# A decoder block on one core: the first weight groups of each half in another order

## The chip, the core and the metric

The kernel runs on one core of one Trainium2 chip. Its engines are TensorE (PE in the rows, with PEld for its weight loads), VectorE (DVE), ScalarE (ACT), GpSimd (POOL) and SyncE (SP), which here only issues transfers. The metric is device time in microseconds, the median of the runs; a profiled execution of the same program gives the trace. In the rows, "A<-B" is an instruction or a transfer that writes tile A and reads B. The kernel records nearly all its instructions through one helper, so the line is L56 almost everywhere, and one goes by the tiles' names.

## What is computed

A decoder trunk of one layer on 2048 tokens of width 1024, in float32:

```python
u = x * (1.0 + scale) + shift                      # from SiLU(c) @ w_ada + b_ada
q, k, v, a_gate, p_in, p_gate, m_a, m_p = split(u @ w_in)
a = sliding_window_sink_attention(q, k, v, ...) * silu(a_gate)
a = a @ w_attn_proj
p = einsum('bsgc,gcd->bsgd', multiscale_causal_pool(p_in), w_pool_mix)
p = ((p * pool_scale) * silu(p_gate)) @ w_pool_proj
y = sigmoid(m_a) * a + sigmoid(m_p) * p
y = (y @ w_out) * (1.0 + gate)
x = layer_norm(alpha * x + y)
```

16 query heads of 64 share two key and value heads; the window is 128 tokens.

## The kernel before

*Products.* Every large matrix product goes in blocks of two by two, with seven products of half-size blocks in place of eight (class `Quad`: two weight tiles of 128 output columns, one chunk of 1024 tokens). The seven are named after the token-side operand: B11, T1, T2, B21, T3, B22, T4. Each float32 operand is split into a high and a low part, and each product is 12 matmuls of 128 x 512 (four blocks, three matmuls each). The weight-side sums are made on GpSimd (`sum1`, `mid`, `late`) and stored to a DRAM tensor `sums_d` in chunk 0 (`keep_sum`); in chunk 1 a quad that has such sums (`again`) loads them instead.

*Order.* Nothing is scheduled by the machine: `phases` lists groups of one or two quads, `plan` turns them into a fixed list of products, and `run` emits them. A group of two runs F (B11, T1 of the first, then of the second), S (T2, B21), Th (T3, B22) and L (T4): 14 products. The two groups of a start phase are thus products 0 to 13 and 14 to 27. After a product's results are complete, `consume(ph, mi, t, src)` is called for one tile of 128 x 512 (output tile `mi`, token half `t`): for the first quad of a pair after products 5, 8, 9 and 12 of the group, for the second after 7, 10, 11 and 13. `defer(2, f)` puts `f`, mostly a store, into program order two products later, and `at(p, f)` hangs other work at product p. Every engine, and SP's queue of transfers, works in program order.

*The start phases.* For each of the two chunks of 1024 tokens (s = 0, 1) a phase with two pairs comes first: `g0` and `g1`. In `g0` the function `head` first makes the modulation and the token-side operands while the data arrives, and does the F and S products of the first pair by hand along the way; so the second quad of the first pair never calls `keep_sum` there, and has no kept sums in chunk 1 either. Between products 10 and 25 of `g0` the function `fold_parts` puts 16 small products (12 matmuls of 128 x 256, into the banks `pv` and `pt` in turn) which fold the pooling weights: ScalarE copies each result to a tile `st`, SP stores it to `wmix_d`. `gate_modulation` fetches 16 half rows of weights (`room_small`) and reduces them on VectorE; its last store is `gate_d`, 4 KB in pieces of 4 bytes.

*What the consumers use.* They take tiles from a ring `c` of the phase (`ph.c`): four tiles in `g0`, six in `g1`. In `g0` the head takes three of them for rows of x. A tile can be written again when the store that reads it has landed.

- `kv_quad`: keys into halves of `spare`, values through a transpose; no tile of `c`.
- `q_quad`: two tiles (`q_hi` on ScalarE, `q_lo` on VectorE), two stores of 256 KB to `q_d`.
- `gate_quad`: one tile `sig` (tanh on ScalarE, and one VectorE instruction for the two gates that are SiLU), one store of 256 KB to `gates_d`, in the rows `ag_d` (attention) and `pg_d` (pooling).

*After the start.* Phase `o0` or `o1` runs 13 quads one at a time and lays attention over them, in steps called every few matmuls. On entry it loads keys (`kk`), the first query tile (`qs`, from `q_d`), the bias (`bt`) and the values (`vv`); later steps load one further query tile for every two steps.

Of the kernel before, what the change touches and what calls it, by code (L numbers as in the profile page):

```python
# [36 lines left out]
TQ, TK, TV, TAG, TPG, TMA, TMP = 0, 8, 9, 10, 18, 26, 34  # L37
# [22 lines left out]
def kernel(  # L60
# [77 lines left out]
    sums_d = dp.tile([36, P, 2, CH], F32, name="sums_d")  # L138
    y_d = dp.tile([S // P, P, KT, P], F32, name="y_d")

    def cols(t, n):
        return t[:, n * CH : (n + 1) * CH]
# [4 lines left out]
    def as32(ap):  # L147
        return ap.bitcast(F32)

    def low(engine, dst, src, hi):  # L150
        engine.tensor_tensor(dst, src, as32(hi), ALU.subtract)
# [9 lines left out]
    def bank(tag="mm"):  # L161
        if tag in ("c1", "pv"):
            return phase_ps["now"].tile([P, CH], F32, tag=tag, bufs=phase_ps["pv"] if tag == "pv" else 1, name=tag)
        return ps.tile([P, CH], F32, tag=tag, bufs=4 if tag == "mm" else 1, name=tag)
# [148 lines left out]
    def defer(ticks, f, local=False):  # L313
        due.append((now[0] + ticks, len(due), f, local))
# [231 lines left out]
    def kv_quad(s):  # L546
        def keep_k(ph, t, src):
            hi, lo = ph.pair()
            act.copy(hi, src)
            low(dve, lo, src, hi)  # L550
            defer(2, lambda: [sp.dma_start(cols(k_d[s, :, n, :], t), as32(x)) for n, x in enumerate((hi, lo))])

        def turn_v(ph, t, vt):
            vtp = bank(("pv", "pt")[t]).rearrange("p (b a d) -> p b a d", b=NB, a=2)
            for b in range(NB):
                pe.transpose(vtp[:, b].rearrange("p a d -> p (a d)"), vt[:, b * P : (b + 1) * P], ident)
            v = ph.two_halves()
            hi, lo = (v.rearrange("p (a b n d) -> p n b a d", a=2, b=NB, n=2)[:, n] for n in range(2))
            act.copy(hi, vtp)
            low(dve, lo, vtp, hi)  # L560
            v = as32(v).rearrange("p (a b d) -> p a b d", a=2, b=NB)
            defer(2, lambda: [sp.dma_start(v_d[s, :, a, NB * t : NB * (t + 1)], v[:, a]) for a in range(2)])

        def consume(ph, mi, t, src):
            if mi == 0:
                keep_k(ph, t, src)
            else:
                vt = ph.own("vt") if s == 0 else cols(ph.spare(), 0)
                act.activation(vt, src, AF.Copy, scale=0.5)
                defer(2, lambda: turn_v(ph, t, vt))  # L570

        return Quad((win[TK], win[TV]), consume)

    def q_quad(s, m):
        def consume(ph, mi, t, src):
            hi, lo = ph.c("q_hi", F32R), ph.c("q_lo", F32R)
            act.activation(hi, src, AF.Copy, scale=-0.125)
            dve.scalar_tensor_tensor(lo, src, -0.125, as32(hi), ALU.mult, ALU.subtract)
            defer(2, lambda: [sp.dma_start(q_d[s, m + mi, t, n], as32(x)) for n, x in enumerate((hi, lo))])

        return Quad((win[TQ + m], win[TQ + m + 1]), consume, sums_d[1 + m // 2], s == 1)

    def gate_quad(s, name, base, m, full):
        def consume(ph, mi, t, src):
            g = ph.c("sig")
            act.activation(g, src, AF.Tanh, scale=0.5)
            if full:
                dve.scalar_tensor_tensor(g, g, 1.0, src, ALU.add, ALU.mult)
            defer(2, lambda: sp.dma_start(gates_d[name][s, m + mi, t], g))

        kept = () if base + m == TAG else (sums_d[5 + (base + m - TAG) // 2], s == 1)
        return Quad((win[base + m], win[base + m + 1]), consume, *kept)

    def mix_quad(s, m):
        def consume(ph, mi, t, src):
            x = ph.c("px")
            act.activation(x, src, AF.Copy, scale=psc[:, m + mi : m + mi + 1])
            defer(2, lambda: sp.dma_start(px_d[m + mi, :, (2 * s + t) * CH : (2 * s + t + 1) * CH], x))

        return Quad(tuple(wmix_d[m + i].rearrange("p k d -> p (k d)") for i in range(2)), consume, sums_d[21 + m // 2], s == 1)  # L600
# [560 lines left out]
    def chunk_quads(s):  # L1161
        def gates(name, base, full):
            return {m: gate_quad(s, name, base, m, full) for m in range(0, KT, 2)}

        q = {m: q_quad(s, m) for m in range(0, KT, 2)}
        x = {m: mix_quad(s, m) for m in range(0, KT, 2)}
        ag, pg = gates("ag", TAG, True), gates("pg", TPG, True)
        ma, mp = gates("ma", TMA, False), gates("mp", TMP, False)
        start = [[kv_quad(s), ag[0]], [q[0], pg[0]]]
        alone = [q[2], ag[2], x[0], x[2], q[4], ag[4], x[4], q[6], ag[6], x[6], pg[2], ma[0], ma[2]]  # L1170
        end = [[pg[4], pg[6]], [ma[4], ma[6]], [mp[0], mp[2]], [mp[4], mp[6]]]
        return start, [[z] for z in alone], end
# [272 lines left out]
    for s in range(2):  # L1445
        start, alone, end = chunk_quads(s)
        if s == 0:
            phase(Pools("g0", spare=2, x=3), start, first_start)
        else:
            phase(Pools("g1", spare=5, wx=2, c=6, ux=2), start, second_start)  # L1450
        phase(Pools(f"o{s}", pv=2, wx=1, p=1, c=5 if s else 4, ux=1), alone, middle(s))
        phase(Pools(f"e{s}", pg=2, wx=2 if s else 3, c=6, ux=1), end, finish_chunk(s, ain_d[0] if s else u1_d))
# [63 lines left out]
```

## Time and profile before

| | |
|---|---|
| median of 3 runs | 1749.45 us (1749.2 to 1755.33) |
| profiled execution, its own time | 1751.48 us |
| its span, first to last instruction | 1749.7 us |
| mean granted TensorE clock | 0.985 |
| TensorE busy | 1672.3 us, 96% of the span |
| VectorE, ScalarE, GpSimd busy | 73%, 54%, 34% |
| transfers | 389.49 MB, mean 223 GB/s |

Busy time of TensorE counts matmuls as they lie in the pipeline, so 96% is not 96% of its peak; but idle time there is time in which the program's order found an operand or a bank not ready. In the profile's rows "idle before" an instruction is followed by what ended it last.

### The profile page before, as it was taken

To read this page: it belongs to the slowest core of one execution; us is meant where nothing else is said; L and a number is where in the kernel's file an instruction comes from. 1 tells how busy PE (TensorE), PEld (TensorE's weight loads), DVE (VectorE), ACT (ScalarE), POOL (GpSimd) and SP (SyncE) were. 2 spreads that over 40 slices of the span, in tenths; PEclk is the share of its full clock that TensorE was granted. 3 is DMA by queue.
4 is the path that set the end of the run, shared out by engine and by line. 5 is a ranking of instruction groups with operands and counts; after the bars stand their busy time and mean duration, and the time that the engine had idled before them with its cause. 6 is when DMAs were issued, how large, how long until landed. Compare 5 with 4: busy or idle time off the path is not lost.

```text
span 1749.7 us, 24770 instructions
## 1 busy us (share of the span) xinstructions
PE 1672.3 (96%) x8061; PEld 1398.1 (80%) x8061; DVE 1278.1 (73%) x2327; ACT 939.7 (54%) x1796; POOL 590.5 (34%) x562
## 2 busy tenths in 40 slices
PE   6889899999999999999999999999999999999996
PEld 5677688888888888888888888888888888888774
DVE  5855677778866778658787887487877785877677
ACT  3644577767763436347767676343545343445441
POOL 3022345454553323323334333322332211123442
PEclk9899999999999999999999999999999999999998
DMA  9388757776647888774556453589957786684342
GB/s 349 106 263 272 205 178 259 215 234 220 203 153 225 264 275 316 264 262 136 165 171 208 152 180 122 195 280 312 348 209 281 249 314 222 221 307 172 144 145 108
DMA packets 237713, 389.49 MB, mean 223 GB/s; under 512 B 21888, under 2 KB 91280, under 8 KB 237456
## 3 DMA queue, kind: packets, MB, share of 16 engines
q1 hardware_dynamic: 236368, 386.29, 66.2%
q10 hardware_dynamic: 1184, 1.60, 0.3%
q8 instruction: 63, 1.03, 0.2%
q14 instruction: 66, 0.54, 0.1%
q0 software_dynamic: 32, 0.02, 0.0%
HBM read 243.63 MB, written 147.35 MB: 223 GB/s over the span
## 4 chain that ended last, share of the span: by engine, by line
PE 63%; DVE 11%; DMA 7%; ACT 6%; issue 5%; POOL 1%; SPq 1%; POOLq 0%; DVEq 0%; ACTq 0%
PE mm L56 38%; PE lg L56 11%; PE c L56 9%; DVE w_set L56 3%; PE pv L56 3%; PE pt L56 2%; DVE L L56 2%; DVE wide L56 2%; ACT L L56 2%; ACT w_set L56 1%; SPq L56 1%; DMA qs<-q_d 1%; DMA wide<-in_xr_dram 1%; DVE p L56 1%; ACT sig L56 1%
## 5 line engine op out<-in xcount | busy, mean ns | idle before, releaser
L56 PE MATMUL mm<-set_B,w_set 128*128 128x512 f32 x2664 | 657.6, 394 | 1.1 <-DVE w_set L56 0.8
L56 PEld LDWEIGHTS mm<-set_B,w_set 128*128 128x128 f32 x2664 | 500.6, 190 | 105.6 <-DVE w_set L56 1.7
L56 POOL TENSOR_TENSOR W<-W 128x512 f32<-128x512 f32 x185 | 267.2, 1454 | 593.0 <-DVE w_set L56 411.6
L56 PE MATMUL mm<-set_T,w_set 128*128 128x512 f32 x1824 | 451.8, 394 | 0.7 <-DVE set_T L56 0.7
L56 PEld LDWEIGHTS mm<-set_T,w_set 128*128 128x128 f32 x1824 | 340.1, 190 | 71.1 <-DVE set_T L56 2.3
L56 DVE TENSOR_TENSOR w_set<-W,w_set 128x1024 fp32r<-128x1024 f32 x198 | 255.9, 1292 | 115.7 <-ACT w_set L56 112.5
L56 ACT CAST w_set<-W 128x1024 fp32r<-128x1024 f32 x222 | 232.1, 1047 | 82.2 <-PE mm L56 52.0
L56 ACT ACTIVATE L<-L 128x257 f32<-128x257 f32 (+3 forms) x384 | 191.2, 500 | 118.7 <-DVE L L56 118.0
L56 PE MATMUL lg<-set_T,w_set 128*128 128x512 f32 x864 | 213.3, 395 | 6.3 <-ACT w_set L56 3.6
L56 PE MATMUL c<-set_T,w_set 128*128 128x512 f32 x864 | 212.9, 395 | 5.1 <-ACT w_set L56 3.0
L56 PEld LDWEIGHTS lg<-set_T,w_set 128*128 128x128 f32 x864 | 163.2, 190 | 43.8 <-ACT w_set L56 4.8
L56 PEld LDWEIGHTS c<-set_T,w_set 128*128 128x128 f32 x864 | 163.3, 190 | 42.1 <-ACT w_set L56 4.6
L56 POOL TENSOR_TENSOR W<-W,A 128x512 f32<-128x512 f32 x41 | 58.0, 1415 | 278.1 <-DMA A<-in_win_dram 128.9
L56 DVE CUSTOM_DVE_ANT_0 L<-lg,bt,nsink 128x256 f32<-128x256 f32 (+1 forms) x256 | 111.0, 469 | 20.7 <-PE lg L56 14.5
L56 PEld LDWEIGHTS lg<-kk,qs 128*128 128x128 f32 x512 | 76.6, 189 | 43.0 <-DVE L L56 26.6
L56 PE MATMUL lg<-kk,qs 128*128 128x256 f32 (+1 forms) x512 | 83.5, 285 | 24.7 <-DVE L L56 18.1
L56 DVE TENSOR_TENSOR ptl<-pt,pth 128x512 fp32r<-128x512 f32 (+1 forms) x128 | 85.7, 670 | 28.8 <-ACT pth L56 27.8
L56 DVE TENSOR_SCALAR L<-L 128x256 f32<-128x256 f32 (+1 forms) x128 | 98.4, 769 | 4.5
L56 ACT ACTIVATE sig<-mm 128x512 f32<-128x512 f32 x76 | 45.5, 599 | 91.4 <-PE mm L56 86.8
L56 ACT CAST pth<-pt 128x512 fp32r<-128x512 f32 (+1 forms) x128 | 72.3, 565 | 20.1 <-PE pv L56 19.1
L56 POOL TENSOR_TENSOR w_set<-W,w_set 128x1024 fp32r<-128x1024 f32 x24 | 58.2, 2424 | 56.6 <-ACT w_set L56 35.3
L56 PE MATMUL pt<-ident,L 128*128 128x128 f32 x496 | 76.9, 277 | 0.0
(203 smaller groups left out, 1938.8 us busy)
## 6 DMA issues: line engine op xcount, KB each, us to landing
W<-in_win_dram SPq DMA_DIRECT2D x40, 512.0 KB, 5.9
qs<-q_d SPq DMA_DIRECT2D x128, 128.0 KB, 4.4
sums_d<-W SPq DMA_DIRECT2D x62, 256.0 KB, 4.0
W<-sums_d SPq DMA_DIRECT2D x31, 512.0 KB, 3.6
ain_d<-st SPq DMA_DIRECT2D x56, 256.0 KB, 3.8
A<-in_win_dram SPq DMA_DIRECT2D x42, 256.0 KB, 5.5
ag_d<-sig SPq DMA_DIRECT2D x32, 256.0 KB, 4.6
q_d<-q_hi SPq DMA_DIRECT2D x32, 256.0 KB, 3.7
```

Of the source, the lines that this page charges most:

```text
L56: return lambda *args, **kw: self.tc.keep_in_program_order(op(*args, **kw))
```

## The change

Each half's first four quads come in another order: the keys and values are paired with the first two query tiles, and the first tiles of both gates form the second pair. Before, keys and values were paired with the attention gate, and the queries with the pooling gate. So that the right sums are kept, the quad that now stands in the head (the queries) has none, and the attention gate's first quad keeps them in chunk 0 and reads them in chunk 1.

```diff
--- before.py
+++ after.py
@@ -578,7 +578,8 @@
             dve.scalar_tensor_tensor(lo, src, -0.125, as32(hi), ALU.mult, ALU.subtract)
             defer(2, lambda: [sp.dma_start(q_d[s, m + mi, t, n], as32(x)) for n, x in enumerate((hi, lo))])
 
-        return Quad((win[TQ + m], win[TQ + m + 1]), consume, sums_d[1 + m // 2], s == 1)
+        kept = (sums_d[1 + m // 2], s == 1) if m else ()
+        return Quad((win[TQ + m], win[TQ + m + 1]), consume, *kept)
 
     def gate_quad(s, name, base, m, full):
         def consume(ph, mi, t, src):
@@ -588,7 +589,7 @@
                 dve.scalar_tensor_tensor(g, g, 1.0, src, ALU.add, ALU.mult)
             defer(2, lambda: sp.dma_start(gates_d[name][s, m + mi, t], g))
 
-        kept = () if base + m == TAG else (sums_d[5 + (base + m - TAG) // 2], s == 1)
+        kept = sums_d[5 + (base + m - TAG) // 2], s == 1
         return Quad((win[base + m], win[base + m + 1]), consume, *kept)
 
     def mix_quad(s, m):
@@ -1166,7 +1167,7 @@
         x = {m: mix_quad(s, m) for m in range(0, KT, 2)}
         ag, pg = gates("ag", TAG, True), gates("pg", TPG, True)
         ma, mp = gates("ma", TMA, False), gates("mp", TMP, False)
-        start = [[kv_quad(s), ag[0]], [q[0], pg[0]]]
+        start = [[kv_quad(s), q[0]], [ag[0], pg[0]]]
         alone = [q[2], ag[2], x[0], x[2], q[4], ag[4], x[4], q[6], ag[6], x[6], pg[2], ma[0], ma[2]]
         end = [[pg[4], pg[6]], [ma[4], ma[6]], [mp[0], mp[2]], [mp[4], mp[6]]]
         return start, [[z] for z in alone], end
```

## The prediction

> **What bounds the kernel now.** I read the page first (busy shares), then what TensorE waits for, by stretch of the span, then the order of time in the two stretches where it waits, and last the windows, for clock and transfers.
>
> The page, its first line and TensorE's entry in part 1:
>
> ```profile
> span 1749.7 us, 24770 instructions
> PE 1672.3 (96%) x8061; PEld 1398.1 (80%) x8061; DVE 1278.1 (73%) x2327; ACT 939.7 (54%) x1796; POOL 590.5 (34%) x562
> ```
>
> TensorE runs 96% of the span, and the change adds and removes no matmul. So only TensorE's idle time, and slow running after it, can move the end. The waits of TensorE, four rows from three answers: the first 200 us, the rest, and the stretch from 686 to 768 us, where chunk 1 opens (engine, what it waited for, total, times, longest):
>
> ```profile
> PE lg L56 <- DMA qs<-q_d: 6.6, 1, 6.6
> PE pv L56 <- ACT st L56: 4.5, 1, 4.5
> PE pt L56 <- ACT st L56: 3.5, 1, 3.5
> ...
> PE lg L56 <- DVE L L56: 16.7, 17, 2.9
> ...
> PE lg L56 <- DVE set_T L56: 0.4, 1, 0.4
> ```
>
> The reader is to see that three single waits stand at the places the change touches: 6.6 at the first score tiles (queries not there), 4.5 in the first group of chunk 0, 3.5 in its second group. After 200 us the largest total is 16.7 in 17 small pieces inside attention, which the order of the start does not touch, and chunk 1's opening has 0.4 us in all, on a set split that stays.
>
> The second group of chunk 0, six rows of the timeline (start, length, engine, operation; in brackets the idle time before it and what ended it):
>
> ```profile
> 145.76 0.33 SPq L56 DMA_DIRECT2D room_small<-in_wada_dram  x1
> 146.14 0.42 SPq L56 DMA_DIRECT2D pg_d<-sig  x1
> 150.30 0.69 DVE L56 SCALAR_TENSOR_TENSOR q_lo<-mm,q_hi 128x512 fp32r<-128x512 f32 x1 [4.57 <-DMA pg_d<-sig]
> 152.66 0.43 SPq L56 DMA_DIRECT2D q_d<-q_hi  x1
> 156.43 0.63 ACT L56 ACTIVATE sig<-p 128x512 f32<-128x512 f32 x1 [8.22 <-DMA q_d<-q_hi]
> 157.58 2.62 PE L56 MATMUL pt<-spare,room_w 128*128 128x256 f32 x12 [3.55 <-ACT st L56]
> ```
>
> This is the ring of four "c" tiles. A query result takes two tiles of it (high and low part), a gate result one, and a tile comes back only when its store has landed. VectorE's q_lo waits 4.57 us for the store of a gate; with VectorE stuck, the fetch behind it on SP's queue is late, and so the next query store (152.66); ScalarE then waits 8.22 us for that store, and with it the copy "st" queued behind, which frees the PSUM bank of the next fold; TensorE idles 3.55 us. What follows it runs slowly. From the chain that ended last, a regular product and fold, then the two products after the stall:
>
> ```profile
> 122.02 2.75 PE lg L56 x12
> 124.77 1.43 PE pv L56 x12
> ...
> 160.20 3.36 PE lg L56 x12
> 163.56 2.73 PE c L56 x12
> ```
>
> **The change part by part.** Products of the two groups are numbered 0 to 27 as in the description above; results of the second member of a pair come at 7, 10, 11, 13 of a group, of the first at 5, 8, 9, 12.
>
> *Group 2 of chunk 0 (removes).* Before: 4 query results x 2 + 4 gate results = 12 tiles through a ring of 4. After: 8 gate results = 8 tiles. So 24 takes the tile of 19, 25 that of 21, 26 that of 22, 27 that of 23: four or five products, at the pace of 2.75 + 1.43 = 4.18 us a product at least 16.7 us, lie between. The tightest I can check in the rows is 25: the store at 146.14 is that of 21's result, it had landed when q_lo ran at 150.30, and product 25 ended at 157.58 - 3.55 = 154.03, so 3.7 us are to spare. I take the whole stall as gone: 3.55 idle, 2.62 - 1.43 = 1.19 on the fold, 3.36 - 2.75 = 0.61 on the product after it; the next one is back at 2.73. Sum **-5.35 us**. Bounds: 0 (another releaser takes over) and -5.35. What is late next: ScalarE's w_set for the following product; it was queued behind the same 8.22 us wait, so it moves with it.
>
> [...] These windows are length, then busy time and count of PE, PEld, DVE, ACT, POOL, granted clock, transfer share, GB/s:
>
> ```profile
> 96.00:100.00 4.00, 1.91 (x15) 1.63 (x13) 0.88 (x3) 0.60 (x1) 0.00 (x0) 1.00 1.02 375
> 156.00:160.00 4.00, 2.42 (x13) 2.42 (x13) 2.91 (x6) 3.54 (x6) 0.25 (x1) 0.75 0.44 137
> 168.00:192.00 24.00, 17.70 (x82) 14.38 (x80) 8.08 (x20) 7.87 (x17) 7.31 (x6) 0.93 1.04 212
> ```
>
> The clock falls to 0.75 in the slice of the stall, and by the chain's rows that costs 1.8 us. [...]
>
> *Group 1 of chunk 0 (adds).* Work on the engines: a query result is one ScalarE and one VectorE instruction, a gate result also. By shape, mean ns behind the bar:
>
> ```profile
> L56 ACT ACTIVATE sig<-mm 128x512 f32<-128x512 f32 x76 | 45.5, 599 | 91.4 <-PE mm L56 86.8 <-issue 4.0
> L56 ACT ACTIVATE q_hi<-mm 128x512 fp32r<-128x512 f32 x22 | 13.2, 599 | 26.5 <-PE mm L56 16.5 <-DMA q_d<-q_hi 9.7
> L56 DVE SCALAR_TENSOR_TENSOR sig<-sig,mm 128x512 f32<-128x512 f32 x40 | 27.5, 686 | 23.6 <-ACT sig L56 23.4
> L56 DVE SCALAR_TENSOR_TENSOR q_lo<-mm,q_hi 128x512 fp32r<-128x512 f32 x22 | 15.2, 692 | 37.8 <-ACT q_hi L56 33.2 <-DMA pg_d<-sig 4.6
> ```
>
> 599 against 599 and 692 against 686: nothing. Transfers (queue, KB each, us to landing, from the page):
>
> ```profile
> ag_d<-sig SPq DMA_DIRECT2D x32, 256.0 KB, 4.6
> q_d<-q_hi SPq DMA_DIRECT2D x32, 256.0 KB, 3.7
> ```
>
> Each of the four results now has two stores of 256 KB instead of one: four more on SP's queue in group 1, four fewer in group 2. Group 1 already has a stall:
>
> ```profile
> 93.95 0.52 SPq L56 DMA_DIRECT2D ag_d<-sig  x1
> 94.97 0.61 SPq L56 DMA_DIRECT2D sums_d<-W  x1
> 95.64 0.64 SPq L56 DMA_DIRECT2D wmix_d<-st  x1
> 96.52 0.60 ACT L56 ACTIVATE sig<-c 128x512 f32<-128x512 f32 x1 [2.25 <-PE c L56]
> 101.72 0.59 ACT L56 COPY st<-pv 128x512 f32<-128x512 f32 x1 [4.60 <-DMA wmix_d<-st]
> 102.36 1.11 PE L56 MATMUL pv<-ident,vt 128*128 128x128 f32 x4 [4.45 <-ACT st L56]
> ...
> 103.47 4.35 PE mm L56 x12
> ...
> DMA to landing us min/median/max: 5.7/5.7/5.7
> ```
>
> (the last row is the landing of the store at 93.95 alone). That store becomes two. The second issue, some 0.5 us, fits between 94.47 and 94.97, where SP waits, so wmix_d is issued no later; but it lands behind 256 KB more. 262,144 bytes at the 375 GB/s of the window from 96 to 100 are 0.70 us: **+0.70 us** on TensorE. Bounds: 0 (queue not full) and 1.4 (the extra store at product 7 still weighs too). The other three extra issues fall where SP waits for VectorE to free a buffer. The new wait in this group: the result of 13 takes tiles whose stores were issued at 93.95 and about 94.4; landing 5.7 later, plus 0.7 behind its own double, by 100.8. ScalarE has only the copy at 101.72 behind it, which the same queue moves to 102.4; 0.6 for q_hi fits. Cost 0 with about 1 us to spare; that cover is the opposite rival's place.
>
> *Start of attention, chunk 0.* Rows of the timeline, and one of the chain:
>
> ```profile
> 168.37 1.14 SPq L56 DMA_DIRECT2D kk<-k_d  x2
> 173.69 0.38 SPq L56 DMA_DIRECT2D gate_d<-mod  x1
> 178.54 1.59 SPq L56 DMA_DIRECT2D qs<-q_d  x2
> ...
> 192.32 1.19 PE L56 MATMUL lg<-kk,qs 128*128 128x256 f32 x4 [6.62 <-DMA qs<-q_d]
> ...
> 179.53 12.70 DMA qs<-q_d
> ```
>
> The query tiles it waits for were written in time even before (product 19); they are late because the load, issued at 179.53, takes 12.70 us behind a full queue (share 1.04 at only 212 GB/s from 168 to 192; the store of the gate vector at 173.69 is in front of it). So the earlier queries buy nothing here by themselves. kk, gate_d and qs are all issued after product 27, so they move by the same 5 us as TensorE, and the wait stays 6.6: **0**. Bounds: +2.9, if the queue cannot start earlier (rival A); -3.6, if the 1 MB fewer in group 2 (4 stores at 294 GB/s, the mean of the 375 and 212 above) empties it sooner (rival B).
>
> *Chunk 1 and the kept sums.* The ring has 6 tiles there, and the opening lost 0.4 us in all. For the first group's queries the sums are now made anew and for the first attention gate read back; before it was the other way round. Same instructions on POOL, VectorE and ScalarE in the same places of their queues, and the same transfers on SP's, from other rows of a tensor: 0, from -0.4 (that wait goes too) to +0.4 (it doubles).
>
> Sum: -5.35 + 0.70 + 0 + 0 = **-4.65 us**. The profiled execution took 1751.48 us, 1.78 outside its span of 1749.7; it would take 1746.8. It lies 2.03 above the median of the three runs, 1749.45, so the median of the changed kernel should be **1744.8 us**.
>
> **The rivals.**
>
> A, the gain is lost at the queue: the transfers between 168 and 192 are the limit, not their issue. For it: share 1.04. Against: 0.44 from 156 to 160, so the queue does empty in the stall and can start earlier. Then qs lands earlier only by the two stores (0.5 MB) that no longer stand just ahead of it: 524,288 bytes at 294 GB/s are 1.8 us. 1749.45 - 1.8 = 1747.7.
>
> B, the wait for qs shrinks as well: 1 MB less, 3.6 us. For it: everything issued there lands in a full queue. Against: most of the megabyte leaves before 160. 1744.8 - 3.6 = 1741.2.
>
> C, the other side: ScalarE's wait in group 1. If the queries' stores issued at 93.95 land later than some 7 us (94.4 + 7 + 0.6 for q_hi, about 102), the result of 13 holds up the copy that TensorE waits for, one for one. It decides against the change once they take over 11.7 us (7 + 4.65). A load in this kernel took as long as this, behind the gate vector (to landing, minimum, median, maximum of the qs loads):
>
> ```profile
> DMA to landing us min/median/max: 2.6/4.4/13.4
> ```
>
> With 13.4: 6.4 more, 1744.8 + 6.4 = 1751.2. Against it: the landing was 5.7.
>
> D, the change doesn't do what it should: the ring was not the releaser. The copy "st" also needs its own buffer back from a store on the same queue, and SP's order there is unchanged. Then the stall stays and group 1 pays: 1749.45 + 0.7 = 1750.2. Against: both waits in the rows name the ring's stores.
>
> E, the clock: the product after the stall of group 1 took 4.35 instead of 2.75, 1.6 us. If the two stalls that stay are each followed by twice that, 1744.8 + 3.2 = 1748.0. [...]
>
> **How the numbers follow.** Forecast 0.52 (its own range 1742.5 to 1747), A 0.12, B 0.14, C 0.06, D 0.08, E 0.08. The time is the forecast's, 1744.8. The range 1740.2 to 1750.4 takes in A, D, E and the near half of B; it leaves out C and the far half of B, 0.13, and some scatter of the runs. A measurement here can tell about 0.5%, 8.7 us: faster means below 1740.7, which is the far half of B and a tail of the forecast, 0.13; slower means above 1758.2, the far end of C with a mishap in chunk 1, 0.04; the rest, 0.83, is no change by that bound.
>
> **What the changed profile would show.** Right: in the second group no wait on a store by sig or VectorE, folds 4.18 us apart throughout, TensorE's wait for "st" of 3.5 gone; kk issued about 4.7 us earlier (near 163.7); the wait for qs between 5.6 and 7.6 and its end near 187.6; the copy at 101.72 about 0.7 later; chunk 1's opening as dense as before. Wrong: a wait of q_hi on q_d ahead of that copy (C), kk early and qs still near 191 (A), the fold still late behind "st" (D), or qs early by 8 (B).

## The result, and the profile after

| | before | after |
|---|---|---|
| median of 17 runs, taken together | 1751.1 us | 1747.3 us (1743.55 to 1751.47) |
| ratio, 95% interval | | **0.9978** (0.9967 to 0.9988) |
| profiled execution, its own time | 1751.48 us | 1747.71 us |
| span | 1749.7 us | 1745.6 us |

The changed kernel is faster by 0.22%: 3.9 us, 2.1 to 5.8 by the interval. It ran again beside the later experiments: 1744.49 against 1748.85 us, ratio 0.9978 (0.9961 to 0.9995). The page of the profile after:

```profile
span 1745.6 us, 24773 instructions
PE 1669.1 (96%) x8061; PEld 1395.7 (80%) x8061; DVE 1278.4 (73%) x2327; ACT 939.9 (54%) x1796; POOL 590.0 (34%) x562
```

TensorE has the same 8061 matmuls. What changed is where it stood still. Group 2 of chunk 0 in the timeline after (start, duration, engine; in brackets the idle time ahead and what ended it):

```profile
140.89 1.59 PE L56 MATMUL pt<-spare,room_w 128*128 128x256 f32 x12
...
149.25 1.59 PE L56 MATMUL pt<-spare,room_w 128*128 128x256 f32 x12
...
154.35 0.63 ACT L56 ACTIVATE sig<-p 128x512 f32<-128x512 f32 x1 [2.41 <-DVE p L56]
...
157.61 1.59 PE L56 MATMUL pt<-spare,room_w 128*128 128x256 f32 x12
157.81 0.60 ACT L56 ACTIVATE sig<-mm 128x512 f32<-128x512 f32 x1 [1.83 <-PE mm L56]
```

The folds into `pt` stand 8.36 us apart throughout, two products of 4.18. ScalarE's results wait for TensorE or VectorE, none for a store. The stall is gone whole. To weigh it free of everything earlier, take the stretch from the fold behind product 14 to the start of product 27, in before, after, and the second profile of after:

```profile
107.66 1.59 PE L56 MATMUL pv<-spare,room_w 128*128 128x256 f32 x12
...
163.40 2.88 PE L56 MATMUL c<-set_T,w_set 128*128 128x512 f32 x12
```
```profile
111.37 1.63 PE L56 MATMUL pv<-spare,room_w 128*128 128x256 f32 x12
...
161.79 2.88 PE L56 MATMUL c<-set_T,w_set 128*128 128x512 f32 x12
```
```profile
105.48 1.59 PE L56 MATMUL pv<-spare,room_w 128*128 128x256 f32 x12
...
155.87 2.88 PE L56 MATMUL c<-set_T,w_set 128*128 128x512 f32 x12
```

That is 55.74 us before, 50.42 and 50.39 after: -5.32 and -5.35.

But 161.79 is only 1.6 us ahead of 163.40. In this execution the changed kernel had lost 3.7 us by the end of group 1 (111.37 against 107.66): 1.4 ahead of its first fold (83.26 against 81.82), which no view here explains, and 2.3 in the group. Group 1 in the first profile of after, timeline and windows (busy us of each engine, then the granted clock):

```profile
101.47 0.60 ACT L56 ACTIVATE q_hi<-c 128x512 fp32r<-128x512 f32 x1 [3.44 <-DMA q_d<-q_hi]
...
104.69 0.59 ACT L56 COPY st<-pv 128x512 f32<-128x512 f32 x1 [2.62 <-DMA wmix_d<-st]
...
105.33 1.12 PE L56 MATMUL pv<-ident,vt 128*128 128x128 f32 x4 [3.66 <-ACT st L56]
```
```profile
84.00:92.00 8.00, 7.26 (x26) 6.32 (x27) 4.99 (x9) 2.84 (x6) 1.29 (x1) 0.57 0.97 315
104.00:112.00 8.00, 6.67 (x22) 5.51 (x23) 3.70 (x6) 3.50 (x6) 2.39 (x2) 0.57 0.71 234
```

and in the second profile of the same program:

```profile
98.01 0.60 ACT L56 ACTIVATE q_hi<-c 128x512 fp32r<-128x512 f32 x1 [5.31 <-DMA q_d<-q_hi]
...
100.00 0.59 ACT L56 COPY st<-pv 128x512 f32<-128x512 f32 x1 [1.40 <-DMA wmix_d<-st]
...
100.64 0.68 PE L56 MATMUL pv<-ident,vt 128*128 128x128 f32 x4 [4.32 <-ACT st L56]
```
```profile
84.00:92.00 8.00, 8.00 (x49) 7.05 (x48) 5.49 (x7) 5.38 (x9) 2.31 (x2) 1.00 0.97 328
```

TensorE's wait for `st` is 3.66 and 4.32 us, no longer than the 4.45 before. What made group 1 of the first profile 2.3 us longer is slow running: the clock was 0.57 from 84 to 92 us, where the same instructions had 1.00 in the second profile, and 0.57 again from 104 to 112, behind the stop. The start of attention, first profile, then second:

```profile
167.27 1.26 SPq L56 DMA_DIRECT2D kk<-k_d  x2
...
172.84 0.38 SPq L56 DMA_DIRECT2D gate_d<-mod  x1
...
192.12 1.19 PE L56 MATMUL lg<-kk,qs 128*128 128x256 f32 x4 [7.55 <-DMA qs<-q_d]
```
```profile
160.96 1.53 SPq L56 DMA_DIRECT2D kk<-k_d  x2
...
166.92 0.38 SPq L56 DMA_DIRECT2D gate_d<-mod  x1
...
184.69 1.19 PE L56 MATMUL lg<-kk,qs 128*128 128x256 f32 x4 [6.55 <-DMA qs<-q_d]
```

In the second profile this matmul runs 7.6 us earlier than before (192.32), with the wait as long as ever (6.55; 6.62 before): it moved along. In the first it ran only 0.2 us earlier. The 4.1 us by which that span is shorter come from places after 1000 us, far behind both openings: set matmul against matmul, 1.5 us near 1070 and 3.5 between 1690 and 1720. The last place is no work of the order: the kernel before with a late gate store (below) runs 3.1 us shorter there too.

### The profile page after: what moved, and what is told of

It is laid out like the page before. It is cut to its first block, busy times and chain, and to the rows that moved or that the text cites. A ratio compares the mean times of both kernels' runs of the same rounds, so it can differ in the third digit from the quotient of the medians.

```text
span 1745.6 us, 24773 instructions
## 1 busy us (share of the span) xinstructions
PE 1669.1 (96%) x8061; PEld 1395.7 (80%) x8061; DVE 1278.4 (73%) x2327; ACT 939.9 (54%) x1796; POOL 590.0 (34%) x562
## 4 chain that ended last, share of the span: by engine, by line
PE 67%; DVE 10%; ACT 6%; issue 5%; DMA 5%; POOL 1%; SPq 1%; POOLq 0%; DVEq 0%; ACTq 0%
PE mm L56 41%; PE lg L56 12%; PE c L56 9%; DVE w_set L56 3%; PE pv L56 3%; PE pt L56 3%; DVE L L56 2%; DVE wide L56 2%; ACT L L56 2%; ACT w_set L56 1%; DMA q_d<-q_hi 1%; DMA vv<-v_d 1%; DVE p L56 1%; ACT sig L56 1%; ACT q_hi L56 1%
## 5 line engine op out<-in xcount | busy, mean ns | idle before, releaser
L56 DVE CUSTOM_DVE_ANT_0 L<-lg,bt,nsink 128x256 f32<-128x256 f32 (+1 forms) x256 | 111.1, 470 | 18.6 <-PE lg L56 11.7
L56 PEld LDWEIGHTS lg<-kk,qs 128*128 128x128 f32 x512 | 76.5, 189 | 43.5 <-DVE L L56 25.3
L56 ACT CAST pth<-pt 128x512 fp32r<-128x512 f32 (+1 forms) x128 | 72.3, 565 | 19.3 <-PE pv L56 18.4
L56 PE MATMUL pv<-pth,vv 128*128 128x256 f32 x248 | 74.9, 323 | 1.9 <-DMA vv<-v_d 1.9
```

The costliest lines, as they stand in the source:

```text
L56: return lambda *args, **kw: self.tc.keep_in_program_order(op(*args, **kw))
```

## The experiments

The same four stretches of TensorE, from the traces of all kernels, in us. Group 1 is from the first fold (81.82 before) to the fold behind product 14; group 2 as above; attention's start from product 27 to the matmul at 192.32 before; the rest to TensorE's last instruction.

| kernel | group 1 | group 2 | attention's start | rest | ratio to before |
|---|---|---|---|---|---|
| before | 25.8 | 55.73 | 28.9 | 1541.6 | |
| new order in chunk 1 only | 25.4 | 55.56 | 28.7 | 1542.2 | 0.9995 |
| before, late gate store | 23.3 | 55.73 | 22.6 | 1553.8 | 1.0018 |
| after | 28.1 | 50.42 | 30.3 | 1538.1 | 0.9978 |
| after, second time | 24.7 | 50.39 | 28.8 | 1542.6 | 0.9978 |
| new order in chunk 0 only | 22.6 | 50.39 | 28.8 | 1542.1 | 0.9949 |
| the same, second time | 24.4 | 50.38 | 28.9 | 1539.9 | 0.9973 |
| after, late gate store | 25.6 | 50.38 | 23.0 | 1550.1 | 0.998 |
| after, gate store on ScalarE's queue | 25.1 | 50.39 | 30.3 | 1541.6 | 0.9987 |
| chunk 0 only, the same gate store | 23.0 | 50.39 | 30.2 | 1541.0 | 0.9985 |
| after, double query stores | 26.0 | 50.39 | 29.1 | 1542.7 | 0.9987 |
| after, two tiles, one store | 24.3 | 50.38 | 30.3 | 1542.5 | 0.998 |
| after, one tile, two stores | 24.9 | 50.39 | 36.4 | 1539.8 | 1.0021 |
| after, two tiles, two stores | 25.3 | 54.91 | 37.3 | 1538.0 | 1.0051 |

**Chunk 0 alone.** After, with the old order for s = 1:

```diff
         start = [[kv_quad(s), q[0]], [ag[0], pg[0]]]
+        if s == 1:
+            start = [[kv_quad(s), ag[0]], [q[0], pg[0]]]
```

> The new order in chunk 0 only; chunk 1 keeps keys and values with the attention gate. If the gain is the stall of the second group of chunk 0, as the prediction has it, all of it is here: ratio to before 0.9965 to 0.999 like the whole change (0.9978), the wait of TensorE for 'st' near 157 us absent, chunk 1 opening with under 1 us of TensorE waits. If the gain came from chunk 1, the ratio is 1.000. The wait for the query tiles near 185 to 192 us: if the load's issue sets it, it stays 6 to 7 us and ends earlier by what TensorE is early; if the full queue sets it, it ends near 192 us whatever TensorE does before, and grows by what TensorE is early.

Measured 1741.4 us (5 runs), ratio 0.9949 (0.9935 to 0.9963), 5 us more of a gain than the whole change. Only chunk 1's order is that of before here: as in the changed kernel, its attention gate reads kept sums and its queries make theirs anew. The gain is larger than that of the full change, so it ran again:

> The new order in the first chunk alone, a second time. It took 1741.4 us (ratio 0.9949) where the full change took 1744.5 to 1747.3, while with the gate's store on the other queue the same two orders gave 0.9985 and 0.9987. If the second chunk's new order costs nothing (theory), the ratio is now 0.997 to 0.999, as that of the full change; if it costs 3 to 5 us, the ratio is again near 0.995.

Measured 1743.95 us (12 runs), ratio 0.9973 (0.996 to 0.9986): that of the full change. The 5 us more did not repeat, so they are no effect of the order; what set the first five runs apart is not known. In the traced one of them, what it won beyond the 5.35 us of group 2 was won ahead of the fold behind product 14, in part behind the stop (3.25 us to that fold, 4.84 in the second series): the granted clock was 1.00 in all slices of 4 us from 80 to 112 us of that trace, where before had 0.50 from 100 to 104 and 0.65 from 104 to 108.

**Chunk 1 alone.** Before, with the new order for s = 1 only:

```diff
         start = [[kv_quad(s), ag[0]], [q[0], pg[0]]]
+        if s == 1:
+            start = [[kv_quad(s), q[0]], [ag[0], pg[0]]]
```

> The new order in chunk 1 only; chunk 0 as before. By the prediction nothing: ratio 0.9993 to 1.0007, the 3.5 us wait for 'st' near 157 us and the 6.6 us wait for the query tiles both there as before. If the whole change owes its gain to chunk 1 (queries stored and loaded back earlier), ratio 0.998 and a shorter start of attention near 769 us.

Measured 1749.01 us, ratio 0.9995 (0.9985 to 1.0006): nothing. Here the sums are those of before (queries read, attention gate makes), so this run tests the order alone; with the new sums the order is tested by the full change beside chunk 0 alone, 0.9978 and 0.9973. No run changes the sums alone. Chunk 0 has the old stall, here in its timeline:

```profile
155.98 0.63 ACT L56 ACTIVATE sig<-p 128x512 f32<-128x512 f32 x1 [8.01 <-DMA q_d<-q_hi]
...
157.13 2.13 PE L56 MATMUL pt<-spare,room_w 128*128 128x256 f32 x12 [3.33 <-ACT st L56]
```

**The gate vector's store later**, in after and in before:

```diff
-        at(base + 26, gate_out)
+        at(base + 60, gate_out)
```

> The changed kernel with the store of the gate vector (4 KB in pieces of 4 bytes, landing 16 us after its issue) moved from 26 to 60 products after the base, far behind the first score tiles. If the full queue behind that store sets the wait for the query tiles, the wait falls from 7.5 us to under 2 and the whole from 0.9978 to 0.993 to 0.996 of before, some 6 us under the changed kernel. If the load's own issue and the other transfers set it, the wait stays over 4 us and the time is within 2 us of the changed kernel. The later place may cost up to 2 us in attention.

> The kernel before with the same late store of the gate vector. The wait for the query tiles falls from 6.6 us likewise. Together with the run of the changed kernel with the late store it gives the worth of the order alone once that queue is out of the way: 5 us (4.65 by the prediction's sum) if the queue was taking some of the gain back; 3.9 us, as measured with the store in its place, if it was not.

Measured 1746.97 us, ratio 0.998 (0.9968 to 0.9991), and 1752.6 us, 1.0018 (1.0004 to 1.0033). The gain of 6 us expected of the first did not come. The wait at the start of attention goes, in both, and comes back near 320 us, where the store now stands ahead of another query load. TensorE's waits in after with the late store, up to 200 us and from there to 480:

```profile
PE lg L56 <- DMA qs<-q_d: 0.7, 1, 0.7
...
PE lg L56 <- DMA qs<-q_d: 5.7, 1, 5.7
```

In before with the late store the wait near 320 us is 6.2 us. So these 4 KB cost some 6 us of waiting at both places tried, and the earlier queries buy nothing by themselves. Between 300 and 345 us the two traces lose 7.3 (after) and 8.7 us (before) against that of before with the store in its place; 5.7 and 6.2 us of that are the wait, and where the rest went was not shown. So the later place gains nothing. With the store late on both sides the order still gains: 1.0018 to 0.998; the two intervals are too wide to tell 3.9 us from 5.

**The same store from ScalarE's queue**, in after and in the order for chunk 0 alone:

```diff
-            sp.dma_start(gate_d.rearrange("k p -> p k"), mod[:, 2 * KT :], allow_slow_non_contiguous=True)
+            act.dma_start(gate_d.rearrange("k p -> p k"), mod[:, 2 * KT :], allow_slow_non_contiguous=True)
```

> The changed kernel with the store of the gate vector (4 KB in pieces of 4 bytes, near 173 us) issued by ScalarE's queue instead of SP's. Theory 1 (the pieces hold up what stands behind them on the same queue): the wait for the first query load at the start of attention falls from 7.5 us to under 2, no new wait appears near 320 us, and the time is 5 to 7 us under the changed kernel, ratio about 0.994 to before. Theory 2 (the pieces occupy the engines, whatever queue they come from): the wait stays at 6 to 8 us and the time is that of the changed kernel.

> The new order in the first chunk alone, with the gate vector's store on ScalarE's queue. The kernel with the new order in the first chunk alone took 1741.4 us, 3 to 5 under the full change, though the new order in the second chunk alone took nothing (ratio 0.9995). If the second chunk's new order costs something when the first chunk's is there too, this kernel lies 3 to 5 us under the other kernel with the gate on ScalarE's queue; if that difference was one of clock and run, the two lie within 1.5 us.

Measured 1747.33 us, ratio 0.9987 (0.9972 to 1.0002), and 1746.32 us, 0.9985 (0.9972 to 0.9998). The wait is still 7.8 us, as theory 2 had it, but it comes by a way that neither theory named. Timeline of the changed kernel with the store on the other queue:

```profile
181.64 0.90 SPq L56 DMA_DIRECT2D W<-wmix_d  x2
...
183.23 1.28 SPq L56 DMA_DIRECT2D qs<-q_d  x2
...
188.71 1.20 PE L56 MATMUL lg<-kk,qs 128*128 128x256 f32 x4 [7.83 <-DMA qs<-q_d]
```

SP stood 11.7 us ahead of the first row, until the store, issued at 167.07, had landed at 181.56. So the query load went out 24.9 us behind the start of product 27 (158.36) instead of 15.5 (second profile of after), and then landed in 5 us instead of 12. In the traces of before and after the landings of SP's 1261 transfers and of ScalarE's 9 are counted on the same eight semaphores, and none of SP's 1257 that reuse one went out before the last transfer on it had landed. That the store and `W<-wmix_d` share one here is the author's reading; no view shows it. In after SP waits for the landing of this store as well: 3.8 us in the first profile, ahead of the eighth issue behind it, and in the second the eighth issue goes out at 181.06, when the store had landed at 181.00. For the query load this pair of kernels therefore does not part the two theories. The load of the values tells more. Transfers issued near 167 us with the store on the other queue (issues: count, KB each, median us to landing), and the same two in after:

```profile
vv<-v_d SPq DMA_DIRECT2D x1, 512.0 KB, 13.5
...
gate_d<-mod ACTq DMA_DIRECT2D x1, 4.0 KB, 14.5
```
```profile
vv<-v_d SPq DMA_DIRECT2D x1, 512.0 KB, 7.7
...
gate_d<-mod SPq DMA_DIRECT2D x1, 4.0 KB, 16.2
```

The values' load, issued beside the store (167.09) on a queue without it, took 13.5 us; in after, where it stands 2.3 us ahead of the store on the same queue, it took 7.7. So here another queue is no shelter from the pieces. That the two kernels lie 0.0002 apart is the second sign that chunk 1's order costs nothing.

**Is it the ring?** Three kernels put back, in group 2 of chunk 0, what the queries had there: two tiles a result, two stores a result, or both. The condition `m == 0` holds for the first quad of both gates, so each edit takes in all eight results, where before only the four query results had two tiles and two stores; the expectations of the second and third kernel speak of the attention gate alone, which is not what their edits do. Before, group 2 had 12 tiles and 12 stores; the changed kernel has 8 and 8. A second tile, stored once (16 tiles, 8 stores):

```diff
-                dve.scalar_tensor_tensor(g, g, 1.0, src, ALU.add, ALU.mult)
+                two = s == 0 and m == 0
+                out_g = ph.c("sig2") if two else g
+                dve.scalar_tensor_tensor(out_g, g, 1.0, src, ALU.add, ALU.mult)
+                g = out_g
```

> The changed kernel, with the first results of both gates in the first chunk written by VectorE to a second tile of the ring c instead of the same one: the instructions and stores are as they were, only each of these gates takes two tiles of the ring, as the queries do. Theory (the ring of four c tiles with their stores was what stopped the second group): the stall comes back in the second group, 3 to 5 us, ratio about 1.000 to 1.001 to before. Rival (the copy st or the stores themselves were the cause): the second group stays without a stall and the ratio is that of the changed kernel, 0.998.

Measured 1745.63 us, ratio 0.998 (0.9969 to 0.999): no stall, as the rival had it, and the expectation of the theory failed. Its timeline shows why:

```profile
153.75 1.59 PE L56 MATMUL pt<-spare,room_w 128*128 128x256 f32 x12
...
156.77 0.69 DVE L56 SCALAR_TENSOR_TENSOR sig<-sig,mm 128x512 f32<-128x512 f32 x1 [3.59 <-DMA ag_d<-sig]
```

The ring's wait is back, but only on VectorE, and behind the last fold: ScalarE's tile is not stored, so ScalarE waits on no result's store there (none among its waits from 112 to 162 us), and the copy `st` behind it is on time. Two more kernels therefore vary tiles and stores apart (`more_d` is a spare tensor). Two tiles, both stored (16 tiles, 16 stores):

```diff
+            first = s == 0 and m == 0 and full
+            out = ph.c("sig2") if first else g
             if full:
-                dve.scalar_tensor_tensor(g, g, 1.0, src, ALU.add, ALU.mult)
-            defer(2, lambda: sp.dma_start(gates_d[name][s, m + mi, t], g))
+                dve.scalar_tensor_tensor(out, g, 1.0, src, ALU.add, ALU.mult)
+            if first:
+                defer(2, lambda: sp.dma_start(more_d[mi, t], g))
+            defer(2, lambda: sp.dma_start(gates_d[name][s, m + mi, t], out))
```

> The changed kernel, where each first result of the attention gate in the first chunk takes two tiles of the ring c and both are stored (ScalarE's tile to a spare tensor in DRAM, VectorE's as before): in tiles and stores the second group is what it was before the change, but without the queries. With a second tile alone (stored once) the ring's wait came back only on VectorE, 3.59 us, and held up nobody. Theory: with ScalarE's own tile stored too, ScalarE waits on a store again in the second group, the copy st stands behind it, and TensorE stops for 3 to 4 us near 155 to 160 us, with the slow fold and product behind the stop; 4 to 6 us over the changed kernel, ratio about 1.000. Rival (the queries' own work in the second group made the stall, not tiles and stores): no stop, ratio 0.998.

Measured 1758.43 us, ratio 1.0051 (1.0033 to 1.007). One tile, stored twice (8 tiles, 16 stores):

```diff
+            if s == 0 and m == 0 and full:
+                defer(2, lambda: sp.dma_start(more_d[mi, t], g))
             defer(2, lambda: sp.dma_start(gates_d[name][s, m + mi, t], g))
```

> The changed kernel, where each first result of the attention gate in the first chunk is stored twice from its one tile of the ring (the second copy to a spare tensor in DRAM): the second group moves as many bytes as before the change, but takes one tile a result. If the bytes on the queue alone made the stall, TensorE stops near 155 to 160 us as in the kernel before (3 to 4 us; ratio about 1.000). If it takes both the two tiles and the stores (theory), a result has four results' time for its store, no engine waits on a store there, and the ratio stays at 0.998 (at most +0.001 by the 1 MB more ahead of the loads of attention).

Measured 1752.02 us, ratio 1.0021 (1.0005 to 1.0037). Timeline of two tiles, two stores:

```profile
148.82 0.60 ACT L56 ACTIVATE sig<-mm 128x512 f32<-128x512 f32 x1 [5.75 <-DMA more_d<-sig]
...
149.94 1.69 PE L56 MATMUL pv<-spare,room_w 128*128 128x256 f32 x12 [1.36 <-ACT st L56]
...
155.86 0.63 ACT L56 ACTIVATE sig<-p 128x512 f32<-128x512 f32 x1 [4.93 <-DMA more_d<-sig]
...
157.02 1.70 PE L56 MATMUL pt<-spare,room_w 128*128 128x256 f32 x12 [2.63 <-ACT st L56]
```

and of one tile, two stores, with the longest of SP's waits behind it (total, times, longest):

```profile
153.58 1.59 PE L56 MATMUL pt<-spare,room_w 128*128 128x256 f32 x12
...
158.82 0.60 ACT L56 ACTIVATE sig<-lg 128x512 f32<-128x512 f32 x1 [3.02 <-DMA ag_d<-sig]
...
170.08 1.15 SPq L56 DMA_DIRECT2D kk<-k_d  x2
...
178.64 1.09 PE L56 MATMUL lg<-kk,qs 128*128 128x128 f32 x4 [6.42 <-DMA qs<-q_d]
```
```profile
SPq L56 <- DMA more_d<-sig: 4.0, 2, 3.8
```

With both, the chain of before is back link by link: ScalarE on a store, `st` behind ScalarE, the fold behind `st`, 1.36 + 2.63 = 3.99 us of TensorE, and group 2 at 54.91 instead of 50.39. With either alone group 2 keeps 50.38 or 50.39; ScalarE's one wait with the stores alone, 3.02 us, came behind the last fold. That settles the releaser: tiles and stores together. It does not give the size, since the 16 stored tiles are more than the 12 of before.

Both kernels with extra stores cost beyond that, which I had put at no more than 0.001 for 1 MB; the eight stores are 2 MB. Their attention starts 6 to 8 us later. In the kernel with one tile, SP issues kk 12.3 us after product 27 begins (170.08, product at 157.76), in the second profile of after 5.1 (160.96 - 155.87). 3.8 of the 7.2 us are SP standing at the landing of an extra store, and that wait is of the edit's own making: `more_d` has four places for eight results, and the pooling gate's last store (issued at 169.18) overwrites what the attention gate's last one (issued at 164.12, landed at 169.10) has just written. So the cost of more stores alone is smaller than these two times say.

**Twice the queries' stores in group 1.**

```diff
+            if s == 0 and m == 0:
+                defer(2, lambda: [sp.dma_start(q_more[mi, t, n], as32(x)) for n, x in enumerate((hi, lo))])
```

> The changed kernel with each store of the first queries in the first chunk (group 1, 8 of 256 KB) issued a second time, to a spare tensor in DRAM. Each extra store in front of the copy's releaser wmix_d was priced at 0.70 us. By that price the wait of st on wmix_d and with it TensorE's stop near 102 us grow by 1.4 to 2.8 us, ratio about 0.999. The rival for this group: ScalarE's wait for the query tiles (q_hi on q_d, 3.4 to 5.3 us, ended 1.4 to 2.6 us ahead of the copy in the two profiles of the changed kernel) takes over as the releaser; then the copy starts right behind q_hi and the stop grows by more, 3 to 6 us, ratio about 1.000 to 1.001.

Measured 1747.0 us, ratio 0.9987 (0.9975 to 0.9999). The place in its timeline:

```profile
100.52 0.60 ACT L56 ACTIVATE q_hi<-c 128x512 fp32r<-128x512 f32 x1 [6.27 <-DMA q_more<-q_hi]
...
102.33 0.58 ACT L56 COPY st<-pv 128x512 f32<-128x512 f32 x1 [1.22 <-DMA wmix_d<-st]
...
102.97 1.05 PE L56 MATMUL pv<-ident,vt 128*128 128x128 f32 x4 [5.09 <-ACT st L56]
```

The stop is 5.09 us, 0.8 to 1.4 over the two profiles of after (4.32, 3.66), less than the 1.4 to 2.8 expected, and only 0.3 over the longest stop of the other kernels with the new group 1 (4.81). The copy is still released by `wmix_d`, and q_hi still lies ahead of it.

## Why the prediction was right

It said 1744.8 us and -4.65 us, in a range of 1740.2 to 1750.4; 1747.3 lies in it, 2.5 above. Of these 2.5, 1.65 are the base (1751.1 over 17 runs, 1749.45 over the three shown), and the rest, 0.8, is within the interval. The range also holds 1749.45, the time of before itself, so the time alone proves little, and that it came so near is in part luck, since one term of the sum is not shown. The stretches say more. By its steps:

- *Group 2, -5.35*: shown. -5.32 and -5.35, and 50.38 to 50.42 in all ten traces of kernels that kept the cause away. The releaser was named rightly, though a second tile alone does not do it, which the row of ScalarE's 8.22 us (its tile came from a stored q_hi) could have told.
- *Group 1, +0.70*: not shown. The stop, 4.45 before, was 3.66 and 4.32 after; 3.6 and 2.7 us in two more kernels with the old group 1, 3.2 to 4.8 in the eight others with the new one and single query stores. With twice the stores it was 5.09, just above all of these: one trace, which fits the direction and does not show it. The copy, foretold 0.7 us later, came 21.4 and 19.3 us behind the first fold, against 19.9 before. A term of this size drowns in the scatter, since the whole of group 1 took 22.6 to 28.1 us. Without the term the forecast is -5.35, which the interval (-5.8 to -2.1) allows as well.
- *The new wait of q_hi on q_d* came as said, 3.44 and 5.31 us, and hid as said: it ended 2.6 and 1.4 us ahead of the copy (104.69 - 102.07; 100.00 - 98.61), where about 1 was foretold.
- *Start of attention, 0*: shown in the second profile and twice with chunk 0 alone: 28.8, 28.8 and 28.9 us against 28.9. In the first it took 30.3, and 30.2 to 30.3 in three of the later kernels, two of them with the gate's store on the other queue; what makes the two values was not settled.
- *Chunk 1, 0*: shown, to the width of the intervals: 0.9995 for the order with the old sums, and 0.9978 beside 0.9973 with the new ones. The sums were not changed alone, but nothing of them is to be seen: in the two traces of after TensorE waits 0.6 and 0.4 us in all from 686 to 768 us, against 0.4 before.

Of the rivals, A (lost at the queue) is refuted by the second profile, where the wait ended 7.6 us earlier and the stretch up to it was as long as before. B (the wait shrinks) did not happen, though 2 MB more there did cost, in part by a wait of their own: the queue was free enough that less bought nothing, yet not so free that more cost nothing. C's wait stayed covered. D (another releaser) fell with the kernel of two tiles and two stores. E had its mechanism and size about right but not its place or its sign: the clock moved group 1 of single executions by 2 to 3 us, after the stall and where there was none, in both directions (3 us longer in the first profile, granted 0.57 from 84 to 92 us; 2 us shorter behind the stop in the first trace of chunk 0 alone, granted 1.00 there). Two things it said one profile would show, the early kk (near 163.7) and the wait ending near 187.6, the first profile did not show (167.27 and 192.12); the second did, at 160.96 and 184.69, with 2.2 us gained at the fold behind product 14 as well.

## What to carry to other kernels

Where results leave through a ring of tiles, count tiles a result times the time of a store against the pace of the results: pairing a consumer of two stored tiles with one that takes none of the ring removed a stall whole, with the same work. Judge a change of a few us by the stretch between two named instructions, which repeated to 0.04 us, not by a profile's total: the two of after differ by 3.0 us (1745.6 and 1742.6). And ask of an engine that waits which in-order work stands behind it: VectorE's wait of 3.59 us behind the last fold cost nothing, ScalarE's of 8.22 ahead of a copy that a fold needed cost 5.3 us. An experiment that adds stores needs a place of its own for each: here two stores to one place added a wait that the question did not hold.

## What was not expected of the hardware

One program, two executions: from 84 to 92 us the clock was 0.57 in one and 1.00 in the other, for the same instructions, and group 1 took 28.1 and 24.7 us. The 3.4 us between the two are 0.2% of 1745, and still as much as the whole change brought.

Ahead of attention a store of 4 KB in pieces of 4 bytes took 13.8 to 16.2 us to land, and a 512-KB load issued beside it from another queue 13.5, where it took 7.7 when it went ahead.

Such a slow store also held up issues that have nothing to do with it: with the gate's store on ScalarE's queue, SP went 11.7 us without an issue until that store had landed (181.56), and its next one, at 181.64, reads another tensor; in after it waited 3.8 us for the same store.
